# Edge scatter by sorting on one Trainium2 core: a new list of sort passes without a rotation of single columns, and smaller last pieces

## The chip, the cores and the metric

The kernel runs on one core of one Trainium2 chip. The metric is the device time of one execution in microseconds (us), taken as the median of the runs. Lower is better.

## What is computed

The reference is a message-passing step on a graph of 4096 nodes with 256 features and 262144 edges:

```python
self_out = nodes @ w_self
src_feat = nodes[edges_src]
msg = src_feat @ w_msg
agg = np.zeros((N, D), dtype=np.float32)
np.add.at(agg, edges_dst, msg)
return (self_out + agg).astype(np.float32)
```

The inputs are drawn with one fixed seed, so that the list of edges is always the same.

## The kernel before

The kernel never gathers rows. It counts, for each pair of source and destination, how many edges there are, and multiplies the counts with `Y = nodes @ w_msg`. For that the edges must be ordered, so that 128 consecutive ones fall into a narrow range of (block of 128 sources, destination). It has three stages.

**Keys and sort.** VectorE (DVE) packs each edge into one fp32 key. The 262144 keys lie as 128 partitions by 2048 columns. The table `SORT_A` is a list of compare-exchange passes `('b', m, parity)`, done by DVE (`mm`, L974: one minimum and one maximum per pass) between two buffers `XA`. In a pass of distance `m` a block of `b` columns is compared with the block `m` columns on, where `b` is the largest power of two that divides `m`. Distances over 96 go through `far_gap`, seven instructions for both parities; the rest through `near`. Between them stand the entries `('q', bb, amounts)`: TensorE (PE) rotates groups of `bb` columns over the partitions, each group by its own amount (`rotate`, L1091 to L1107). A rotation has two halves of 1024 columns. A half is two PSUM tiles of 4 groups, each filled by 4 matmuls of 128 columns in fp32 (the trace shows each as two; L1100) and copied back by ScalarE (ACT, L1104). There are eight rotations; this text calls them turns 0 to 7. The ninth `q` is done by `relayout`.

The order around a turn is written out by hand in `near`. The last two passes before a turn are done first for the first half of the columns, so that PE can turn it while DVE finishes the second half. After the turn the first two passes are done first for the first half, while PE turns the second. `warm` (L994) puts matmuls on zeros in front of a turn, each burst of three tied to a DVE instruction a given number of us ahead (`WARM`, one entry per turn). Between turns PE also does independent work (`early`: transposes, the projection `Y`, and the rows `nodes @ w_self`).

**Tail and values.** `relayout` spreads the keys anew, `tail` runs the passes of `SORT_S` on the first half of the edges (buffers `XS`); the second half (`XR`) is sorted during the main loop. PE then transposes the sorted keys and subtracts a base (L453, L462), and ACT turns the result into the int16 `vals` (L467, two instructions of 512 columns). DVE's first use of them is `pair` (L536).

**Main loop.** 2048 columns of 128 edges each, in 37 groups. `GROUPS` gives for each group the number of columns, the width `wid` of its one-hot of destinations, and the largest step to the next column. DVE (and ACT for a part, L592) builds one-hots `e_oh` (sources) and `d_oh` (destinations, `wid` wide, L601). PE multiplies them into `ring` (L628: 128 by `wid` counts a column; also 352 clearing matmuls with `zer`), ACT copies finished runs to `atr` (L655), DVE adds the spill between runs (L688), and PE multiplies the counts with `Y` (L718, L725). The wider a group, the more columns each of its matmuls and one-hots has. If one column of edges spans more than its `wid`, a flag sends the program to a slow loop over all edges at the end (`_any_edges`).

Of the kernel before, what the change touches and what calls it, by code (L numbers as in the profile page):

```python
# [9 lines left out]
P = 128  # L10
FP32 = mybir.dt.float32
# [8 lines left out]
ACTF = mybir.ActivationFunctionType  # L20
# [1 line left out]
BW = 512  # L22
SEG = 384
SHORT = 256
W = 92
NC = 64
GROUPS = [
# [7 lines left out]
]  # L35
PARTS = 2
LATE = (7, 17)
# [7 lines left out]
BEFORE, AFTER = 1, 3  # L45
FP = 96
BP = 128
WARM = [((2.7, 1.4), 3)] * 4 + [((1.6,), 3), ((2.7, 1.4), 3), ((1.6,), 3), ((1.6,), 3), ((2.7, 1.4), 3)]
FILLS = (24, 10, 10, 10, 0, 5, 0, 0, 5)
LAG = (16, 56)  # L50
RAMP = (64, 384)
# [15 lines left out]
PIECES = (512, 512, 480, 320, 224)  # L67
TOP = 32767
SORT_A = [
    ('b', 419, 0),  # L70
    ('b', 419, 1),
    ('b', 287, 0),
    ('b', 287, 1),
    ('b', 343, 0),
    ('b', 343, 1),
    ('b', 175, 0),
    ('b', 175, 1),
    ('b', 141, 0),
    ('b', 141, 1),
    ('b', 97, 0),  # L80
    ('b', 97, 1),
    ('b', 49, 0),
    ('b', 49, 1),
    ('q', 32, [108, 126, 61, 93, 118, 18, 115, 104, 48, 77, 58, 46, 7, 70, 116, 61]),
    ('b', 49, 0),
    ('b', 49, 1),
    ('b', 25, 0),
    ('b', 25, 1),
    ('q', 16, [91, 19, 26, 97, 35, 114, 42, 89, 83, 23, 118, 3, 50, 4, 17, 64]),
    ('b', 35, 0),  # L90
    ('b', 35, 1),
    ('b', 19, 0),
    ('b', 19, 1),
    ('q', 8, [116, 58, 105, 69, 107, 57, 36, 32, 125, 115, 105, 36, 76, 85, 65, 104]),
    ('b', 11, 0),
    ('b', 11, 1),
    ('b', 10, 0),
    ('b', 10, 1),
    ('q', 2, [2, 29, 75, 18, 94, 19, 8, 3, 68, 97, 94, 43, 15, 42, 52, 96]),
    ('b', 6, 0),  # L100
    ('b', 6, 1),
    ('q', 2, [110, 57, 19, 3, 2, 47, 70, 27, 104, 50, 9, 91, 21, 61, 124, 94]),
    ('b', 5, 0),
    ('b', 5, 1),
    ('b', 3, 0),
    ('b', 3, 1),
    ('q', 2, [65, 105, 76, 15, 103, 58, 124, 82, 97, 61, 78, 40, 33, 44, 18, 114]),
    ('b', 2, 0),
    ('b', 2, 1),
    ('q', 1, [49, 55, 109, 124, 1, 37, 105, 21, 18, 46, 96, 19, 46, 41, 31, 24]),  # L110
    ('b', 2, 0),
    ('b', 2, 1),
    ('q', 2, [19, 54, 43, 88, 45, 89, 44, 103, 107, 0, 94, 90, 82, 64, 24, 26]),
    ('b', 2, 0),
    ('b', 2, 1),
    ('b', 1, 0),
    ('b', 1, 1),
    ('q', 1, [48, 125, 14, 17, 54, 81, 102, 117]),
]
SORT_S = [  # L120
    (54, 0), (54, 1), (62, 0), (62, 1), (38, 0), (38, 1), (26, 0), (26, 1), (18, 0), (18, 1), (14, 0), (14, 1), (8, 0), (8, 1),
]


# [5 lines left out]
def kernel(  # L130
# [9 lines left out]
    nc = tc.nc  # L140
# [24 lines left out]
    GP = G16 // PARTS  # L165
# [52 lines left out]
    for h, m in enumerate(PIECES):  # L218
# [4 lines left out]
        q = nc.scalar if h < 4 else nc.sync  # L223
# [15 lines left out]
    for d64, s64, c in ld:  # L239
# [5 lines left out]
            out=seg[:, c], in_=dlo, func=ACTF.Copy, scale=1.0 / SEG, bias=0.5 / SEG - 6.5  # L245
        )
        nc.scalar.activation(
            out=blk[:, c], in_=slo, func=ACTF.Copy, scale=1.0 / P, bias=0.5 / P - 0.5
        )
        loaded = nc.scalar.activation(  # L250
            out=dst_p[:, c], in_=dlo, func=ACTF.Copy, scale=1.0 / (SEG - SHORT), bias=0.0
# [196 lines left out]
    tps = []  # L448
# [11 lines left out]
    for t, tp in enumerate(tps):  # L460
        for k in range(4):
            nc.tensor.matmul(  # L462
                out=tp[:, k * P:(k + 1) * P],
                lhsT=g7f[:, 4 * t + k:4 * t + k + 1].to_broadcast([P, P]), rhs=ident[:],
                start=False, stop=True, skip_group_check=True,
            )
        nc.scalar.activation(  # L467
            out=vals[:].rearrange("p (q k) -> p q k", k=GP)[:, :, 4 * t:4 * t + 4],
            in_=tp[:].rearrange("p (k q) -> p q k", k=4),
            func=ACTF.Relu, scale=-1.0, bias=top[:],  # L470
        )

    def load(c):
        regs = [nc.tensor.alloc_register(f"po{c}_{i}") for i in range(NREG)]
# [488 lines left out]
class _Sort:  # L963
# [127 lines left out]
    def rotate(self, x, y, bb, rots):  # L1091

        for h in range(2):
            sel = lambda v: v[:, FP + 1024 * h:FP + 1024 * (h + 1)].rearrange(
                "p (i g b) -> p g i b", g=8, b=bb
            )
            for t in range(2):
                tp = self.psum.tile([P, 512], FP32, name="tp_sw", tag="tp", bufs=4)
                for g in range(4):
                    self.nc.tensor.matmul(  # L1100
                        out=tp[:, g * P:(g + 1) * P], lhsT=self.turned(rots[8 * h + 4 * t + g]),
                        rhs=sel(x)[:, 4 * t + g], start=True, stop=True,
                    )
                self.nc.scalar.copy(  # L1104
                    out=sel(y)[:, 4 * t:4 * t + 4],
                    in_=tp[:].rearrange("p (g i b) -> p g i b", g=4, b=bb),
                )  # L1107

    def run(self, fill, more):
# [109 lines left out]
```

## Time and profile before

| | us |
|---|---|
| median of 3 runs | 419.08 (418.66 to 419.38) |
| profiled execution | 418.17 |
| its span, first to last instruction | 416.4 |
| around the span | 1.8 |
| busy DVE, PE, ACT, POOL in the span | 374.9, 335.5, 270.0, 43.0 |
| mean granted clock of TensorE | 0.978 |

The profiled execution is 0.91 us under the median. An engine's busy time says little by itself here, since DVE is busy for 90% of the span and PE for 81%, each the bound in another stage. What counts is which of them the others wait for, stretch by stage.

### The profile page before, as it was taken

The page shows a single profiled execution, that of the slowest core. Times are in us where ns is not written, and L with a number is a line of the kernel's source. Part 1 is how long each engine was busy: PE and PEld are TensorE (multiplying, and loading weights), DVE is VectorE, ACT ScalarE, POOL GpSimd, SP SyncE. Part 2 cuts the span into 40 slices and gives each one's busy share as a digit, 9 for nine tenths or more (in the row PEclk, how much of TensorE's full clock was granted, in tenths as well). Part 3 has the DMA queues.
Part 4 walks back from the last instruction along what each step waited for, and adds up shares of the span by engine and source line. Part 5 has one row for each costly group of instructions (what it writes and reads, how often), then busy time and mean ns, then how long its engine had stood idle before and what let it go on. Part 6 is the DMA issues. An engine that isn't in the chain of part 4 may idle for free.

```text
span 416.4 us, 10756 instructions
## 1 busy us (share of the span) xinstructions
PE 335.5 (81%) x4128; PEld 287.9 (69%) x4137; DVE 374.9 (90%) x916; ACT 270.0 (65%) x559; POOL 43.0 (10%) x172
## 2 busy tenths in 40 slices
PE   0038477876967198999999998898988999999995
PEld 0025255564845056999999998797878988898895
DVE  6999999999799989999999999989997999998851
ACT  4328154553538015889888888996876877777782
POOL 8400000000000000002011020100102030202010
PEclk9999699999999689999999999999999999999999
DMA  8690000101023200003012020230203020211212
GB/s 305 138 185 4 2 1 2 50 0 52 1 101 116 87 0 2 2 2 39 2 16 28 2 32 10 53 41 8 33 3 39 2 32 12 28 14 15 29 16 53
DMA packets 18074, 16.20 MB, mean 39 GB/s; under 512 B 3684, under 2 KB 16997, under 8 KB 18022
## 3 DMA queue, kind: packets, MB, share of 16 engines
q0 software_dynamic: 8992, 6.29, 12.7%
q1 hardware_dynamic: 8310, 7.20, 5.3%
q10 hardware_dynamic: 720, 2.00, 1.2%
q8 instruction: 34, 0.56, 0.6%
q14 instruction: 18, 0.15, 0.1%
HBM read 8.93 MB, written 8.66 MB: 42 GB/s over the span
## 4 chain that ended last, share of the span: by engine, by line
DVE 47%; PE 45%; issue 3%; ACT 3%; DMA 1%; DVEq 0%; ACTq 0%
DVE XA L974 18%; PE out_ps L718 18%; PE ring L628 17%; DVE e_oh L601 7%; PE tp_sw L1100 5%; DVE d_oh L601 5%; DVE XS L974 4%; DVE XR L974 3%; DVE off L564 3%; PE warm L994 2%; PE out_ps L725 1%; DMA d<-in_edges_dst_dram 1%; ACT XA L1104 1%; DVE atr L688 1%; ACT atr L655 1%
## 5 line engine op out<-in xcount | busy, mean ns | idle before, releaser
L655 ACT CAST atr<-ring 128x472 bf16<-128x472 f32 (+11 forms) x352 | 177.2, 553 | 45.7 <-PE ring L628 40.7
L718 PE MATMUL out_ps<-Y,atr 128*128 128x256 bf16 x1024 | 162.2, 272 | 2.9 <-DVE atr L688 2.0
L628 PE MATMUL ring<-d_oh,e_oh 128*128 128x88 bf16 (+9 forms) x2048 | 149.7, 203 | 9.9 <-issue 4.5
L628 PEld LDWEIGHTS <-e_oh 128*128 128x128 bf16 x2048 | 129.2, 97 | 16.4 <-issue 9.7
L718 PEld LDWEIGHTS <-atr 128*128 128x128 bf16 x1024 | 90.7, 97 | 10.8 <-DVE atr L688 2.3
L974 DVE TENSOR_TENSOR XA<-XA 128x510 f32<-128x510 f32 (+30 forms) x154 | 89.3, 630 | 6.9 <-ACT XA L1104 5.3
L601 DVE TENSOR_SCALAR e_oh<-off 128x1024 bf16<-128x1024 int16 (+5 forms) x254 | 87.0, 402 | 7.9 <-PE ring L628 5.2
L628 PE MATMUL ring<-zer 128*128 128x158 bf16 (+12 forms) x352 | 81.4, 231 | 0.1
L866 POOL DMA_DIRECT2D out_dram<-o_sb x30 | 28.9, 963 | 357.8 <-ACT atr L655 357.8
L601 DVE TENSOR_SCALAR d_oh<-off 128x1024 bf16<-128x1024 int16 (+5 forms) x204 | 63.9, 373 | 0.0
L1104 ACT COPY XA<-tp_sw 128x512 f32<-128x512 f32 x32 | 20.9, 654 | 41.5 <-PE tp_sw L1100 41.2
L1100 PE MATMUL tp_sw<-XA,id 128*128 128x128 f32 x256 | 36.7, 298 | 7.9 <-DVE XA L974 7.8
L1100 PEld LDWEIGHTS tp_sw<-XA,id 128*128 128x128 f32 x256 | 33.1, 194 | 13.7 <-DVE XA L974 8.7
L564 DVE TENSOR_TENSOR off<-pair,rows 128x2048 int16<-128x2048 int16 (+5 forms) x34 | 38.6, 1134 | 0.3
L628 PEld LDWEIGHTS <-zer 128*128 128x128 bf16 x352 | 34.1, 97 | 5.0 <-ACT atr L655 1.9
L994 PE MATMUL warm<-zw 128*128 128x512 bf16 x61 | 20.8, 440 | 17.5 <-DVE XS L974 9.3
L349 PE MATMUL x_ps<-id_bf,nodes_bf 128*128 128x128 bf16 x64 | 8.5, 304 | 29.3 <-DMA nodes_bf<-in_nodes_dram 28.0
L725 PE MATMUL out_ps<-Y,atr 128*88 128x256 bf16 (+7 forms) x115 | 31.2, 272 | 0.0
L688 DVE TENSOR_TENSOR atr<-atr 128x178 bf16<-128x178 bf16 (+24 forms) x100 | 23.7, 260 | 6.4 <-ACT atr L655 6.0
L349 PEld LDWEIGHTS <-nodes_bf 128*128 128x128 bf16 x64 | 6.6, 139 | 30.9 <-DMA nodes_bf<-in_nodes_dram 28.3
L321 PE MATMUL y_ps<-wcat,XT 128*128 128x256 bf16 x128 | 21.7, 278 | 6.9 <-ACT Y L325 2.8
L592 ACT ACTIVATE e_oh<-off,onesc 128x512 bf16<-128x512 uint16 (+5 forms) x36 | 24.6, 686 | 2.7 <-DVE off L564 2.7
(114 smaller groups left out, 223.3 us busy)
## 6 DMA issues: line engine op xcount, KB each, us to landing
out_dram<-o_sb POOLq DMA_DIRECT2D x30, 128.0 KB, 3.2
nodes_bf<-in_nodes_dram POOLq DMA_DIRECT2D x2, 1024.0 KB, 12.6
out_dram<-nodes_bf SPq DMA_DIRECT2D x4, 512.0 KB, 2.9
out_dram<-XA SPq DMA_DIRECT2D x4, 512.0 KB, 3.0
d<-in_edges_dst_dram SPq DMA_DIRECT2D x2, 512.0 KB, 5.5
s<-in_edges_src_dram ACTq DMA_DIRECT2D x2, 512.0 KB, 5.7
d<-in_edges_dst_dram SPq DMA_DIRECT2D x1, 480.0 KB, 9.6
s<-in_edges_src_dram ACTq DMA_DIRECT2D x1, 480.0 KB
```

The lines of the kernel that those rows point to most:

```text
L564: tt(out=v[:, 0:n // 2].rearrange("p g w (k i) -> p (g w) k i", i=2), in0=pair[:, g].rearrange("p g w i -> p (g w) i").unsqueeze(2).to_bro ...
L601: ins = tss(out=o[:, 0:n // 2, j:j + m].rearrange("p g k i -> p g (k i)"), in_=v[:, 0:n // 2, w, 0:2 * m], scalar=float((-j0 if w else ON_ ...
L628: mm = nc.tensor.matmul(out=ap, lhsT=lhsT, rhs=rhs, start=start, stop=True, skip_group_check=True,).ins
L655: ins = nc.scalar.copy(out=at[:, 0:n], in_=ring[:, b:b + n]).ins
L688: tt(out=atr[:, j:j + n, 0:m], in0=atr[:, j:j + n, 0:m], in1=atr[:, i:i + n, at:at + m], op=ALU.add,)
L718: nc.tensor.matmul(out=out_ps[:, i, :], lhsT=at[:, t * P:(t + 1) * P], rhs=Y[:, b, :], start=(b == 0 and not last and t % 2 == 0), stop=(b ...
L725: nc.tensor.matmul(out=out_ps[0:m, 0, :], lhsT=spill[:, c0:c0 + m], rhs=Y[:, b, :], start=False, stop=False, skip_group_check=True,)
L866: nc.gpsimd.dma_start(out=dst, in_=src, accum_op=ALU.add).ins,
L974: self.nc.vector.tensor_tensor(out=out, in0=in0, in1=in1, op=op),
L994: self.nc.tensor.matmul(out=w[:], lhsT=self.zw[:, 0:P], rhs=self.zw[:], start=True, stop=True).ins
L1100: self.nc.tensor.matmul(out=tp[:, g * P:(g + 1) * P], lhsT=self.turned(rots[8 * h + 4 * t + g]), rhs=sel(x)[:, 4 * t + g], start=True, sto ...
L1104: self.nc.scalar.copy(out=sel(y)[:, 4 * t:4 * t + 4], in_=tp[:].rearrange("p (g i b) -> p g i b", g=4, b=bb),)
```

## The change

There are five edits. The list `SORT_A` has other distances and amounts (same number of passes and turns), and its turn 6 rotates groups of two columns in place of single ones. `SORT_S` has other distances. `GROUPS` has other widths (from a mean of 86.4 columns to 87.7, and `W`, the widest, from 92 to 94), which follow from the new order of the edges. Each half of a rotation has three PSUM tiles, of 4, 2 and 2 groups, in place of two of 4. The bursts before the turns change: five in front of turn 0 from 6.0 us ahead, and two in front of every other turn, where turns 4, 6 and 7 had one. The activation of `vals` is done in four pieces, the first 32 columns of edges first.

```diff
-W = 92
+W = 94
...
-WARM = [((2.7, 1.4), 3)] * 4 + [((1.6,), 3), ((2.7, 1.4), 3), ((1.6,), 3), ((1.6,), 3), ((2.7, 1.4), 3)]
+WARM = [((6.0, 4.8, 3.6, 2.4, 1.2), 3)] + [((2.7, 1.4), 3)] * 8
+TURNED = ((0, 4), (4, 2), (6, 2))
...
-    ('b', 419, 0),
-    ('b', 419, 1),
...
+    ('b', 812, 0),
+    ('b', 812, 1),
...
-    ('q', 1, [49, 55, 109, 124, 1, 37, 105, 21, 18, 46, 96, 19, 46, 41, 31, 24]),
+    ('q', 2, [64, 80, 21, 16, 104, 59, 44, 35, 47, 1, 40, 49, 125, 101, 28, 24]),
...
-        nc.scalar.activation(
-            out=vals[:].rearrange("p (q k) -> p q k", k=GP)[:, :, 4 * t:4 * t + 4],
-            in_=tp[:].rearrange("p (k q) -> p q k", k=4),
-            func=ACTF.Relu, scale=-1.0, bias=top[:],
-        )
+    for q in (slice(0, 32 // GP), slice(32 // GP, P)):
+        for t, tp in enumerate(tps):
+            nc.scalar.activation(
+                out=vals[:].rearrange("p (q k) -> p q k", k=GP)[:, q, 4 * t:4 * t + 4],
+                in_=tp[:].rearrange("p (k q) -> p q k", k=4)[:, q],
+                func=ACTF.Relu, scale=-1.0, bias=top[:],
+            )
...
-            for t in range(2):
-                tp = self.psum.tile([P, 512], FP32, name="tp_sw", tag="tp", bufs=4)
-                for g in range(4):
+            for g0, n in TURNED:
+                tp = self.psum.tile([P, 512], FP32, name="tp_sw", tag="tp", bufs=4)[:, 0:n * P]
+                for g in range(n):
                     self.nc.tensor.matmul(
-                        out=tp[:, g * P:(g + 1) * P], lhsT=self.turned(rots[8 * h + 4 * t + g]),
-                        rhs=sel(x)[:, 4 * t + g], start=True, stop=True,
+                        out=tp[:, g * P:(g + 1) * P], lhsT=self.turned(rots[8 * h + g0 + g]),
+                        rhs=sel(x)[:, g0 + g], start=True, stop=True,
                     )
                 self.nc.scalar.copy(
-                    out=sel(y)[:, 4 * t:4 * t + 4],
-                    in_=tp[:].rearrange("p (g i b) -> p g i b", g=4, b=bb),
+                    out=sel(y)[:, g0:g0 + n],
+                    in_=tp.rearrange("p (g i b) -> p g i b", g=n, b=bb),
                 )
```

The distances over 96, which set the length of the far passes, were 419, 287, 343, 175, 141, 97 and are 812, 323, 279, 269, 163, 97. The first far passes on DVE, before (the last number is columns, or blocks by columns of a block; `x2` is two equal rows):

```order
L974 TENSOR_TENSOR XA_93<-XA_92 128x815
L974 TENSOR_TENSOR XA_92<-XA_92 128x605
L974 TENSOR_TENSOR XA_93<-XA_92 128x210
L974 TENSOR_TENSOR XA_93<-XA_92,XA_93 128x605 x2
L974 TENSOR_TENSOR XA_93<-XA_92 128x209 x2
L974 TENSOR_TENSOR XA_92<-XA_93 128x881
```

and with the change:

```order
L977 TENSOR_TENSOR XA_93<-XA_92 128x155x4
L977 TENSOR_TENSOR XA_92<-XA_92 128x53x4
L977 TENSOR_TENSOR XA_93<-XA_92 128x102x4
L977 TENSOR_TENSOR XA_93<-XA_92,XA_93 128x53x4 x2
L977 TENSOR_TENSOR XA_93<-XA_92 128x101x4 x2
L977 TENSOR_TENSOR XA_92<-XA_93 128x863
```

The number of instructions is the same; those of the first pair are shorter.

The copies of turns 5 and 6 on ACT, before (`tp_sw` with its number is the PSUM tile; the size is groups by rows of blocks by columns of a block):

```order
L1104 COPY XA0_92<-tp_sw_890 128x4x64x2
L1104 COPY XA0_92<-tp_sw_896 128x4x64x2
L1104 COPY XA0_92<-tp_sw_902 128x4x64x2
L1104 COPY XA0_92<-tp_sw_908 128x4x64x2
L1104 COPY XA1_93<-tp_sw_930 128x4x128
L1104 COPY XA1_93<-tp_sw_936 128x4x128
L1104 COPY XA1_93<-tp_sw_942 128x4x128
L1104 COPY XA1_93<-tp_sw_948 128x4x128
```

and with the change:

```order
L1107 COPY XA0_92<-tp_sw_926 128x4x64x2
L1107 COPY XA0_92<-tp_sw_932 128x2x64x2
L1107 COPY XA0_92<-tp_sw_936 128x2x64x2
L1107 COPY XA0_92<-tp_sw_940 128x4x64x2
L1107 COPY XA0_92<-tp_sw_946 128x2x64x2
L1107 COPY XA0_92<-tp_sw_950 128x2x64x2
L1107 COPY XA1_93<-tp_sw_974 128x4x64x2
L1107 COPY XA1_93<-tp_sw_980 128x2x64x2
L1107 COPY XA1_93<-tp_sw_984 128x2x64x2
L1107 COPY XA1_93<-tp_sw_988 128x4x64x2
L1107 COPY XA1_93<-tp_sw_994 128x2x64x2
L1107 COPY XA1_93<-tp_sw_998 128x2x64x2
```

Turn 6 has the form of turn 5, and the last copy of each half is half as long. PE's own order is unchanged but for the bursts.

## Rows read from the trace of the kernel before

**Rows 1.** Windows by stage: length, then busy PE, PEld, DVE, ACT, POOL, clock, DMA

```profile
19.18:46.65 27.47, 12.09 (x80) 8.42 (x80) 26.92 (x42) 11.53 (x24) 1.15 (x2) 0.94 0.59 77
46.65:126.08 79.43, 62.32 (x391) 46.31 (x397) 72.89 (x125) 35.14 (x76) 0.00 (x0) 0.98 0.08 27
...
202.00:262.00 60.00, 57.58 (x840) 53.43 (x838) 58.43 (x147) 51.09 (x104) 5.46 (x6) 1.00 0.13 17
262.00:411.00 149.00, 139.91 (x2085) 127.69 (x2086) 129.07 (x392) 117.19 (x243) 20.62 (x21) 1.00 0.19 24
```

**Rows 2.** The page's chain that ended last, shares of the span by line

```profile
DVE XA L974 18%; PE out_ps L718 18%; PE ring L628 17%; DVE e_oh L601 7%; PE tp_sw L1100 5%; DVE d_oh L601 5%; DVE XS L974 4%; DVE XR L974 3%; DVE off L564 3%; PE warm L994 2%; PE out_ps L725 1%; DMA d<-in_edges_dst_dram 1%; ACT XA L1104 1%; DVE atr L688 1%; ACT atr L655 1%
```

**Rows 3.** Timeline of DVE between the turns: start, length, work, [idle before it]

```profile
52.57 10.52 DVE L974 TENSOR_TENSOR XA<-XA 128x511 f32<-128x511 f32 x16 [0.66 <-ACT XA L1104]
63.34 10.49 DVE L974 TENSOR_TENSOR XA<-XA 128x511 f32<-128x511 f32 x16 [0.25 <-ACT XA L1104]
...
93.12 7.84 DVE L974 TENSOR_TENSOR XA<-XA 128x515 f32<-128x515 f32 x12 [0.26 <-ACT XA L1104]
101.25 5.56 DVE L974 TENSOR_TENSOR XA<-XA 128x510 f32<-128x510 f32 x12 [0.29 <-ACT XA L1104]
109.09 3.03 DVE L974 TENSOR_TENSOR XA<-XA 128x510 f32<-128x510 f32 x8 [2.28 <-ACT XA L1104]
112.82 5.14 DVE L974 TENSOR_TENSOR XA<-XA 128x510 f32<-128x510 f32 x8 [0.70 <-ACT XA L1104]
118.33 7.84 DVE L974 TENSOR_TENSOR XA<-XA 128x514 f32<-128x514 f32 x12 [0.36 <-ACT XA L1104]
```

**Rows 4.** DVE instructions by form: busy, mean ns of one

```profile
L974 DVE TENSOR_TENSOR XA<-XA 128x976 f32<-128x976 f32 x1 | 1.2, 1177 | 0.0
L974 DVE TENSOR_TENSOR XA<-XA,XA 128x605 f32<-128x605 f32 x2 | 1.6, 788 | 0.0
L974 DVE TENSOR_TENSOR XS<-XS 128x256 f32<-128x256 f32 x4 | 1.5, 420 | 0.0
L601 DVE TENSOR_SCALAR d_oh<-off 128x1024 bf16<-128x1024 int16 x135 | 49.1, 418 | 0.0
```

**Rows 5.** Timeline of PE around turns 1, 4 and 6

```profile
57.97 1.67 PE L994 MATMUL warm<-zw 128*128 128x512 bf16 x5
...
86.42 0.81 PE L994 MATMUL warm<-zw 128*128 128x512 bf16 x3
87.47 2.10 PE L1100 MATMUL tp_sw<-XA,id 128*128 128x128 f32 x16 [0.24 <-DVE XA L974]
...
102.91 0.81 PE L994 MATMUL warm<-zw 128*128 128x512 bf16 x3
104.01 7.65 PE L1100 MATMUL tp_sw<-XA,id 128*128 128x128 f32 x32 [0.30 <-DVE XA L974]
```

**Rows 6.** Timeline of ACT after turn 4: a copy of 512 columns, one of 256

```profile
92.50 0.59 ACT L1104 COPY XA<-tp_sw 128x512 f32<-128x512 f32 x1 [0.25 <-PE tp_sw L1100]
92.98 0.38 ACT L325 COPY nodes_bf<-y_ps 128x256 f32<-128x256 f32 x1
```

**Rows 7.** Windows ahead of turn 0 and turn 5, columns as in rows 1

```profile
41.80:46.60 4.80, 0.00 (x0) 0.00 (x0) 4.70 (x8) 0.37 (x1) 0.00 (x0) 0.67 0.00 0
...
92.30:98.40 6.10, 3.22 (x17) 1.29 (x15) 5.73 (x10) 2.16 (x6) 0.00 (x0) 1.00 0.26 89
```

**Rows 8.** The values: timelines of ACT and DVE, and a short activation by form

```profile
153.12 1.52 ACT L467 ACTIVATE vals<-tp_sw,top 128x512 int16<-128x512 f32 x2 [17.45 <-PE tp_sw L462]
...
154.67 0.18 DVE L536 TENSOR_SCALAR pair<-vals 128x32 int16<-128x32 int16 x1 [1.09 <-ACT vals L467]
...
L498 ACT ACTIVATE rel_q<-XR,g7f 128x128 int16<-128x128 f32 x8 | 2.9, 404 | 0.0
```

**Rows 9.** PE's matmuls into the ring by form: busy, mean ns of one

```profile
L628 PE MATMUL ring<-d_oh,e_oh 128*128 128x83 bf16 x288 | 20.2, 201 | 0.6 <-issue 0.2
...
L628 PE MATMUL ring<-d_oh,e_oh 128*128 128x90 bf16 x192 | 14.5, 205 | 0.3 <-issue 0.2
```

More of the change, by code (lines that the diff above doesn't have):

```diff
@@ L69 @@
 SORT_A = [
-    ('b', 419, 0),
-    ('b', 419, 1),
[L72 to L79, printed above, removed]
+    ('b', 812, 0),
+    ('b', 812, 1),
+    ('b', 323, 0),
+    ('b', 323, 1),
+    ('b', 279, 0),
+    ('b', 279, 1),
+    ('b', 269, 0),
+    ('b', 269, 1),
+    ('b', 163, 0),
+    ('b', 163, 1),
     ('b', 97, 0),
     ('b', 97, 1),
[L82 to L102, printed above, removed]
+    ('b', 54, 0),
+    ('b', 54, 1),
+    ('q', 32, [102, 55, 115, 44, 27, 73, 103, 20, 45, 68, 53, 40, 23, 87, 82, 41]),
+    ('b', 82, 0),
+    ('b', 82, 1),
+    ('b', 51, 0),
+    ('b', 51, 1),
+    ('q', 16, [3, 61, 58, 1, 27, 117, 122, 84, 122, 53, 62, 24, 36, 4, 35, 72]),
+    ('b', 29, 0),
+    ('b', 29, 1),
+    ('b', 21, 0),
+    ('b', 21, 1),
+    ('q', 8, [67, 92, 79, 68, 20, 82, 28, 50, 104, 1, 86, 8, 103, 12, 43, 58]),
+    ('b', 13, 0),
+    ('b', 13, 1),
+    ('b', 9, 0),
+    ('b', 9, 1),
+    ('q', 2, [43, 88, 94, 55, 63, 89, 96, 71, 82, 54, 7, 112, 117, 88, 14, 22]),
+    ('b', 7, 0),
+    ('b', 7, 1),
+    ('q', 2, [118, 5, 84, 86, 8, 61, 102, 88, 87, 50, 27, 114, 111, 40, 66, 10]),
     ('b', 5, 0),
@@ L106 @@
     ('b', 3, 1),
-    ('q', 2, [65, 105, 76, 15, 103, 58, 124, 82, 97, 61, 78, 40, 33, 44, 18, 114]),
+    ('q', 2, [50, 26, 89, 49, 88, 116, 9, 77, 55, 8, 84, 40, 38, 89, 14, 108]),
     ('b', 2, 0),
     ('b', 2, 1),
-    ('q', 1, [49, 55, 109, 124, 1, 37, 105, 21, 18, 46, 96, 19, 46, 41, 31, 24]),
+    ('q', 2, [64, 80, 21, 16, 104, 59, 44, 35, 47, 1, 40, 49, 125, 101, 28, 24]),
     ('b', 2, 0),
     ('b', 2, 1),
-    ('q', 2, [19, 54, 43, 88, 45, 89, 44, 103, 107, 0, 94, 90, 82, 64, 24, 26]),
+    ('q', 2, [52, 47, 92, 72, 102, 25, 97, 88, 110, 3, 59, 101, 35, 54, 99, 120]),
     ('b', 2, 0),
@@ L117 @@
     ('b', 1, 1),
-    ('q', 1, [48, 125, 14, 17, 54, 81, 102, 117]),
+    ('q', 1, [35, 94, 7, 63, 40, 91, 54, 72]),
 ]
 SORT_S = [
-    (54, 0), (54, 1), (62, 0), (62, 1), (38, 0), (38, 1), (26, 0), (26, 1), (18, 0), (18, 1), (14, 0), (14, 1), (8, 0), (8, 1),
+    (42, 0), (42, 1), (70, 0), (70, 1), (34, 0), (34, 1), (30, 0), (30, 1), (18, 0), (18, 1), (14, 0), (14, 1), (8, 0), (8, 1),
 ]
```

14 rows, old and new, of the table GROUPS are left out of this document.

## The prediction

> **What bounds the kernel now.** I read the windows by stage first. Through the sort DVE is busy for 26.92 of 27.47 us while it does the far passes and for 72.89 of 79.43 in the stage of the turns, while PE is busy for less than half of the first and has long gaps in the second; in the main loop DVE leads between 202 and 262 us (58.43 of 60) and PE after that (139.91 of 149, DVE 129.07) [rows 1]. The chain that ended last says the same: the passes on XA and XS and the one-hots are DVE's, `ring` and `out_ps` are PE's, 17% and 18% of the span [rows 2]. So a column less in a DVE pass before 150 us counts in full, and a column more in the ring counts wherever PE leads. Next I read DVE's timeline for the places where the sort does not compute. It idles once per turn, for about 0.25 us (turns 2 and 3 have 0.24 each, as turn 1 has 0.25), for 0.66 at turn 0, and for 2.28, 0.70 and 0.36 around turns 6 and 7, each time until a copy by ACT [rows 3]. PE's timeline gives the cause of the large ones: turn 6, of single columns, takes 32 matmuls in 7.65 us, where a half of another turn takes 16 in 2.10 [rows 5].
>
> **The passes.** The far list loses 962 columns of instructions (21652 before, 20690 now, in 42 instructions both times); the near passes gain 129, the tail 96. A column costs (1177 - 788) / 371 = 1.05 ns [rows 4]. Nothing else runs on that path, so this is 737 x 1.05 = **0.77 us less**. Blocks of four and of two columns replace single ones in some passes. The tail's blocks of eight fall on the same line (420 ns for 256 columns, and 788 - 349 x 1.05 = 422), so for those I take the same price.
>
> **Turn 6.** Between 101.25 and 118.33 us, 17.08 us, DVE waits 2.28 + 0.70 + 0.36 = 3.34 us for copies [rows 3]. Where DVE does not wait, an instruction starts some 0.08 us before the end of the last, which the three waits also cost: 3.6 us in all. With groups of two columns turn 6 is like turn 4, where the first half (from 87.47, 2.10 long) is turned while DVE does the second and DVE does not wait for it. So 3.6 us go, but not all: the bursts. A burst of three issues in 0.64 (five take 1.67 and three 0.81, so 0.215 a matmul). PE does its work in order, and there is little room: at turn 6 the single burst starts at 102.91, so PE is free at 103.55, and the turn is ready at 104.01. Two bursts hold PE until 104.19, 0.18 late [rows 5]. At turn 4 they start at 86.42 and hold PE until 87.70, 0.23 behind the 87.47 at which it could start. At turn 7 the half before the burst starts later by what turn 6 was late, and I get about 0.4. Shorter last copies (next part) take 0.2 back each time; DVE, which comes 0.2 earlier itself, then waits about 0.23 at each of the three. For turns 6 and 7 that leaves 3.6 - 0.45 = **3.15 us less**. The ends: 3.6 if the bursts delay nothing, and 2.6 if each costs a whole burst more.
>
> **Smaller last tiles.** A half's last copy now has 256 columns. A copy of 512 takes 0.59, one of 256 0.38 [rows 6], and the last matmuls of the half end when they did, so DVE goes on 0.2 us earlier, wherever it waits for that copy: turns 0, 1, 2, 3 and 5, 1.0 us. The two more copies per half lie on ACT, which is idle between the copies. At turn 4 the 0.26 of the second half [rows 3] goes with its 0.08, and a wait of 0.23 behind the bursts comes: 0.1. Turn 0 waits 0.4 longer than turn 1, and TensorE ran at the lower of its two levels in part of the stretch before it (mean granted clock 0.67 while PE was idle) [rows 7]. Five bursts from 6 us ahead follow the projection within half a us, so that the long idle stretch is gone; I take the whole 0.4. Together **1.5 us less**; ends 0.6 and 2.0.
>
> **The values.** DVE waits 1.09 us until the second of two activations, 153.12 to 154.64, ends [rows 8]. Now it waits for two pieces of 16 columns. The first is hidden in the time in which ACT waits for the second tile's matmuls. The second takes at most the 0.40 us of the form with 128 columns, in place of 0.69 [rows 8]; the slope between the two gives some 0.3. So **0.4 us less**; ends 0.29 and 0.6. The long pieces end later than before, by about 0.8 us, and DVE needs them only for the second split of `vals`, over 4 us later. [...]
>
> **The wider groups.** The mean width goes from 86.4 to 87.7: 2512 more columns in 2048 matmuls, and 510 more in the clearing ones. By the forms of 83 and 90 columns a column costs (205 - 201) / 7 = 0.57 ns; the two means are rounded, so I take 0.5: 1.5 us on PE [rows 9]. PE leads in about three quarters of the main loop, which makes 1.15. In the rest DVE leads, and of its 2480 more elements of `d_oh` at no more than 418 / 1024 = 0.41 ns [rows 4], 1.0 us, a quarter counts, 0.2. Together **1.3 us more**; ends 0, if all of it falls into the idle 9 us that PE has after 262 [rows 1], and 2.5, if both count everywhere.
>
> **The sum.** -0.77 - 3.15 - 1.5 - 0.4 + 1.3 = -4.5 us. Against the profiled execution's own 418.17 this is 413.7; it stands 0.9 below the median of 419.08, against which it would be 414.6. Part of that 0.9 may be turn 0, whose clock came back just in time in this execution; the change would end that difference. I take 414.1.
>
> **The rivals.** *A low clock at turn 0.* The new bursts come in groups of three with pauses. If the clock falls in spite of them, and is low when turn 0 starts, its matmuls take twice 2.1 us, 2.1 longer than forecast for the first half: 416.2. Against it: between 92.30 and 98.40 PE was busy for 3.22 of 6.10 us with such pauses, and the granted clock stayed at 1.00 [rows 7]; the new bursts make about as much. For it: the clock did fall before turn 0 when PE stood idle. [...] Chance 0.14.
>
> *More is hidden.* The bursts delay nothing (0.7 us) and the wider groups fall into idle time (1.3): 414.1 - 2.0 = 412.1. For it speaks that PE idles 9 us of its own last stage, against it that the chain runs through the ring there [rows 1, 2]. Chance 0.15.
>
> *The table does not fit.* This one ends on the other side. The widths and steps in `GROUPS` are right only for the order that the new list makes of this draw. One column of 128 edges that spans a destination more than its `wid` sets the flag, and the slow loop runs: 2048 rounds. Of each only its DVE instructions, at 0.4 us for a small one [rows 4], would make over 2000 us. It decides at a single column. The list has passes over all distances, the draw is fixed, and the widths that I get by carrying the passes out on that draw are those of the table; so 0.01. That the change does not do what it says otherwise is not possible for the passes, whose lengths are in the program.
>
> **How the numbers follow.** The forecast has 0.68, with 412.9 to 415.6 as its own range from the ends above, of which not all fall on one side. The other case below (0.15) and the low clock (0.14) lie at 412.1 and 416.2; the range of 412.0 to 416.4 takes in both centres and half of what lies beyond. A measurement of this kernel can tell about 0.2%, 0.8 us, from no change. Every case but the last lies more than that below 419.08, so faster has 0.96; 0.02 each are left for no change and for slower, where several small delays and the last rival are.
>
> **What would show it.** Right: far passes that end about 1.0 us earlier; no copy over 0.6 us and 16 matmuls a half at turn 6; DVE waits of about 0.05 us at turns 0, 1, 2, 3, 5 and of about 0.2 at turns 4, 6 and 7, each behind six `warm` matmuls; `pair` 0.4 us nearer to the last subtraction on PE; a main loop about 1.3 us longer from `pair` to the end. Wrong: a granted clock under 1.00 at turn 0, a main loop as long as before or longer by over 2.5 us, or DVE waits at turns 4, 6 and 7 that are gone or over half a us.

## The result and the profile after

The changed kernel takes **408.44 us** (median of four executions, 407.44 to 409.74), the kernel before, run beside it, 418.87 (418.18 to 419.38): a ratio of 0.9754, 95% interval 0.9715 to 0.9792. The forecast was 414.1 with a range of 412.0 to 416.4, so the gain is more than twice the one forecast. The profiled execution took 409.74 us, its span 408.0. It is 1.3 above its median, the one of before (418.17) 0.7 below the 418.87; of the 10.4 us between the medians the two profiles show 8.4. Ratios in this text leave out executions that took over 1.5% longer than the fastest of their kernel, which are two of `e5_before_pad18` and one of `c4_old_lists`.

The windows of the kernel after come first: the far passes and the turns as in [rows 1], then a stretch ahead of turn 0, which answers to [rows 7], and one near the end of the tail. Columns as in [rows 1].

```profile
18.71:45.30 26.59, 15.79 (x88) 9.58 (x89) 26.00 (x43) 11.58 (x24) 0.94 (x2) 1.00 0.60 79
45.30:120.37 75.07, 59.33 (x402) 43.74 (x406) 72.91 (x125) 33.96 (x92) 0.00 (x0) 1.00 0.09 29
38.00:45.40 7.40, 5.94 (x19) 2.09 (x18) 7.26 (x13) 2.27 (x7) 0.00 (x0) 1.00 0.00 0
142.00:144.00 2.00, 1.94 (x7) 0.79 (x6) 1.93 (x7) 0.00 (x0) 0.00 (x0) 0.61 0.00 0
```

The far passes are 0.9 us shorter. Their clock of 1.00 can't be taken at its word: in this trace the clock is on record only from 44.6 us on, and windows show 1.00 for what is not on record. The 512-column matmuls of the bursts start 0.38 to 0.43 us apart up to 44.04 and 0.21 apart from 44.73 on. The trace of before has two levels of the granted clock, 0.50 and 1.00; there such matmuls start 0.38 to 0.43 us apart at 0.50 (43.5 to 50.3 us) and 0.21 apart at 1.00 (from 86.42, ahead of turn 4), so TensorE was at the lower level until about 44.6 and at the higher when turn 0 began, at 48.13. DVE in the stage of the turns is as busy as before (72.91 and 72.89 us) in 4.4 us less. The chain of the kernel after, shares of the span by line, against [rows 2]:

```profile
PE out_ps L721 24%; PE ring L631 23%; DVE XA L977 19%; DVE XS L977 4%; DVE e_oh L604 3%; PE out_ps L728 3%; PE tp_sw L1103 3%; DVE d_oh L604 2%; PE warm L997 2%; ACT XA L1107 2%; DVE off L567 1%; DMA d<-in_edges_dst_dram 1%; DVE XR L977 1%;
```

PE's two lines of the main loop have grown from 35% to 47%. DVE's timeline (start, length, work, idle before it) now has only two waits that the view sets apart, where before it had nine (seven of them in [rows 3]):

```profile
45.06 42.82 DVE L977 TENSOR_TENSOR XA<-XA 128x48 f32<-128x48 f32 x70
88.11 16.01 DVE L977 TENSOR_TENSOR XA<-XA 128x511 f32<-128x511 f32 x28 [0.24 <-ACT XA L1107]
104.39 16.06 DVE L977 TENSOR_TENSOR XA<-XA 128x510 f32<-128x510 f32 x28 [0.27 <-ACT XA L1107]
```

PE's timeline around turns 4 and 6 tells why these two stay. Each follows a turn of 16 matmuls that comes right behind six of `warm`, so PE was late; at turn 6 the 32 matmuls in 7.65 us of [rows 5] have become twice 16 in about 2 us.

```profile
84.22 1.67 PE L997 MATMUL warm<-zw 128*128 128x512 bf16 x6
85.72 1.95 PE L1103 MATMUL tp_sw<-XA,id 128*128 128x128 f32 x16
...
100.44 1.67 PE L997 MATMUL warm<-zw 128*128 128x512 bf16 x6
101.94 1.95 PE L1103 MATMUL tp_sw<-XA,id 128*128 128x128 f32 x16
104.27 2.02 PE L1103 MATMUL tp_sw<-XA,id 128*128 128x128 f32 x16 [0.38 <-DVE XA L977]
```

The values, ACT's timeline, against [rows 8]:

```profile
147.50 0.27 ACT L470 ACTIVATE vals<-tp_sw,top 128x16 int16<-128x16 f32 x1 [17.56 <-PE tp_sw L463]
148.34 0.84 ACT L470 ACTIVATE vals<-tp_sw,top 128x16 int16<-128x16 f32 x2 [0.56 <-PE tp_sw L463]
```

`pair` starts at 148.64 (154.67 before). Counted from the first far pass (18.71; 19.18 before), the sort and the values take 129.93 us in place of 135.49, **5.56 less**. The prediction's first four terms make 5.82. The main loop, from `pair` to the end of the span, takes 259.3 us in place of 261.7: **2.4 less, where 1.3 more was forecast**. So the question is the main loop, in which the change only widened groups.

### The profile page after: what moved, and what is told of

Read it like the earlier page. It is cut to its first block, busy times and chain, and to the rows that moved or that the text cites. A ratio compares the mean times of both kernels' runs of the same rounds, so it can differ in the third digit from the quotient of the medians.

```text
span 408.0 us, 10819 instructions
## 1 busy us (share of the span) xinstructions
PE 336.9 (83%) x4145; PEld 288.6 (71%) x4155; DVE 374.9 (92%) x916; ACT 269.1 (66%) x577; POOL 43.1 (11%) x172
## 4 chain that ended last, share of the span: by engine, by line
PE 55%; DVE 37%; ACT 3%; issue 3%; DMA 1%; DVEq 0%; ACTq 0%
PE out_ps L721 24%; PE ring L631 23%; DVE XA L977 19%; DVE XS L977 4%; DVE e_oh L604 3%; PE out_ps L728 3%; PE tp_sw L1103 3%; DVE d_oh L604 2%; PE warm L997 2%; ACT XA L1107 2%; DVE off L567 1%; DMA d<-in_edges_dst_dram 1%; DVE XR L977 1%; DVE XA L260 1%; DVE XA L255 1%
## 5 line engine op out<-in xcount | busy, mean ns | idle before, releaser
L658 ACT CAST atr<-ring 128x471 bf16<-128x471 f32 (+11 forms) x352 | 177.2, 555 | 43.5 <-PE ring L631 38.3
L631 PE MATMUL ring<-d_oh,e_oh 128*128 128x87 bf16 (+10 forms) x2048 | 150.3, 204 | 5.1 <-DVE d_oh L604 2.0
L977 DVE TENSOR_TENSOR XA<-XA 128x510 f32<-128x510 f32 (+33 forms) x154 | 89.4, 630 | 2.6 <-ACT XA L1107 0.5
L1107 ACT COPY XA<-tp_sw 128x256 f32<-128x256 f32 (+1 forms) x48 | 19.7, 448 | 38.0 <-PE tp_sw L1103 37.7
L1103 PE MATMUL tp_sw<-XA,id 128*128 128x128 f32 x256 | 32.4, 278 | 7.0 <-DVE XA L977 6.5
L1103 PEld LDWEIGHTS tp_sw<-XA,id 128*128 128x128 f32 x256 | 30.0, 190 | 11.3 <-DVE XA L977 9.2
L997 PE MATMUL warm<-zw 128*128 128x512 bf16 x78 | 24.6, 425 | 14.8 <-DVE XS L977 9.4
L728 PE MATMUL out_ps<-Y,atr 128*89 128x256 bf16 (+6 forms) x115 | 31.3, 272 | 0.0
L691 DVE TENSOR_TENSOR atr<-atr 128x174 bf16<-128x174 bf16 (+24 forms) x100 | 23.6, 262 | 5.8 <-ACT atr L658 5.3
L997 PEld LDWEIGHTS <-zw 128*128 128x128 bf16 x87 | 8.4, 104 | 27.7 <-DVE XS L977 9.7
```

Of the source, the lines that this page charges most:

```text
L631: mm = nc.tensor.matmul(out=ap, lhsT=lhsT, rhs=rhs, start=start, stop=True, skip_group_check=True,).ins
L658: ins = nc.scalar.copy(out=at[:, 0:n], in_=ring[:, b:b + n]).ins
L691: tt(out=atr[:, j:j + n, 0:m], in0=atr[:, j:j + n, 0:m], in1=atr[:, i:i + n, at:at + m], op=ALU.add,)
L728: nc.tensor.matmul(out=out_ps[0:m, 0, :], lhsT=spill[:, c0:c0 + m], rhs=Y[:, b, :], start=False, stop=False, skip_group_check=True,)
L977: self.nc.vector.tensor_tensor(out=out, in0=in0, in1=in1, op=op),
L997: self.nc.tensor.matmul(out=w[:], lhsT=self.zw[:, 0:P], rhs=self.zw[:], start=True, stop=True).ins
```

## What the trace of before showed in the main loop

PE's waits of the kernel before from 155 to 412 us (line, what it waited for, total, times, longest), those without a releaser:

```profile
PE ring L628 <- issue: 4.5, 9, 1.2
...
PE out_ps L718 <- issue: 0.4, 1, 0.4
```

And of the kernel after:

```profile
PE out_ps L721 <- issue: 2.3, 4, 1.2
...
PE ring L631 <- issue: 1.6, 4, 0.5
```

"issue" is time in which nothing that the profile knows held PE. One such place of before, in PE's timeline:

```profile
318.34 0.20 PE L628 MATMUL ring<-d_oh,e_oh 128*128 128x89 bf16 x1
319.76 0.38 PE L628 MATMUL ring<-d_oh,e_oh 128*128 128x89 bf16 x5 [1.23 <-issue]
```

It falls inside a row of equal matmuls, and in the trace neither the matmul at 319.76 nor its weight load waits for a semaphore. The queues of the page of before have one that no line of the kernel feeds (packets, MB, share):

```profile
q8 instruction: 34, 0.56, 0.6%
```

These are 34 loads of 16 KB, and PE's program, as compiled, has 8251 instructions, about 243 for each load. In the trace one load lasts from 317.06 to 318.49, and PE goes on at 319.76. I numbered the ring's and `out_ps`'s matmuls by their place in PE's program (weight loads and waits counted too) and took, for each, the time since the start of the one before, less its columns at the rate of the `warm` matmuls at a granted clock of 1.00 (0.21 us for 512) and 5 ns, which are an estimate (ring matmuls of 88 columns start 40 ns apart in the median, 3 more than this rate gives). Places where the profile shows PE waiting for another engine are left out. In the kernel before seven pauses of 0.5 to 1.4 us stand at instructions 4338, 4850, 5363, 5875, 6130, 7154 and 7411: all within 1 of the same remainder, 243, modulo 256. In each of the seven PE goes on 1.17 to 1.49 us after the end of the load that ran just before. I call the places with that remainder borders. Over the 28 borders of the main loop the pauses sum to **7.5 us before and 5.1 after**, which is the 2.4 us by which the loop is shorter. What the change did to them: the ring began at PE's instruction 712 and begins at 749, mostly through the 18 added `warm` matmuls with a weight load each, so every border falls on other work. The traces show this without the numbering: counted from the ring's first matmul, pauses stand before numbers 1747, 2241 and 2488 in the kernel before and before 1730, 2223 and 2470 in the kernel after, 17 or 18 matmuls earlier.

## The experiments

Theory A: the new widths and steps shorten the loop themselves. Theory B: the borders of PE's program moved. Theory C: chance from execution to execution. Later F: the bursts act on the main loop in another way. The pauses, the loop and the clock are read from the one execution of each kernel that was traced; the medians are of all. All ratios are to the kernel before, run beside each. The expectations have 8.8 us of pauses for before, since they count 1.29 at a border (instruction 5108) where PE also waits for DVE; the tables below leave such places out everywhere.

### One part of the change at a time

`e1_lists_only`: the kernel before with `SORT_A`, `SORT_S`, `GROUPS` and `W` of the change.

> The kernel before with the new sort lists, widths and steps, and nothing else of the change. The sort should give 0.8 us for the columns and 3.6 for turn 6, as its bursts stay single: 4.4 less until `pair`. Theory A (the widths and steps of the new table make the main loop shorter): the main loop from `pair` to the end is about 2.4 us shorter, as in the changed kernel, so 6.8 less in all, about 412. Theory B (PE's 36 added instructions ahead of the main loop move its instruction loads, and so its stalls): without them the main loop is longer by up to 1.3, so 3.1 to 4.4 less, 414.5 to 415.8. Theory C (the main loop varies by this much from execution to execution): between the two, with main loops that overlap those of the kernel before.

416.36 us, ratio 0.9944 (0.9926 to 0.9962). The sort and values are 3.6 shorter, the main loop 265.0, 3.3 *longer* than before. Theory A falls.

`e2_old_bursts`: the changed kernel with `WARM` of before.

```
-WARM = [((6.0, 4.8, 3.6, 2.4, 1.2), 3)] + [((2.7, 1.4), 3)] * 8
+WARM = [((2.7, 1.4), 3)] * 4 + [((1.6,), 3), ((2.7, 1.4), 3), ((1.6,), 3), ((1.6,), 3), ((2.7, 1.4), 3)]
```

> The changed kernel with the warming bursts of the kernel before: 18 matmuls fewer, in other places. In the sort turn 0 loses its long burst (0.4 to 0.6 us more, clock low before it), and turns 4, 6 and 7 lose the 0.2 that PE held them up (0.6 to 0.7 less): about even. Theory A: the main loop stays as in the changed kernel, time 408.0 to 409.0. Theory B: the main loop loses its gain of 2.4 us, time 410.5 to 411.5. Theory C: anywhere between.

415.47 us, 0.9913 (0.9889 to 0.9937). Until `pair` it is 0.3 behind the changed kernel, in the main loop (263.9) 4.5. PE's waits in the loop (155 to 412 us):

```profile
PE ring L631 <- issue: 6.8, 11, 1.4
```

`e4_bursts_only`: the kernel before with the new `WARM`.

> The kernel before with the new bursts alone: 36 more PE instructions ahead of the main loop, and the same lists. In the sort turn 0 gains 0.4 to 0.6 (no low clock ahead of it), turns 4, 6 and 7 lose 0.2 each: 0 to 0.2 longer until `pair`. Theory A: main loop as before, 418.9 to 419.2 in all. Theory B: main loop 2.4 shorter or more (the lists cost it 1.3), 415.5 to 417. Theory C: in between.

413.88 us, 0.9872 (0.9846 to 0.9897): half of the whole gain, from bursts that do no work. The sort takes what it took (135.49 us from the first far pass to `pair`, as before), the main loop 257.3, 4.4 less. So the same 18 matmuls are worth 4.4 us in the main loop with the old lists and 4.5 with the new. Theory C falls too: the changed kernel took 407.4 to 409.7 us, with the old bursts 414.6 to 417.0.

B's forecasts for these three had the sign right, but not the size: 414.5 to 415.8 for `e1_lists_only`, 410.5 to 411.5 for `e2_old_bursts`, 415.5 to 417 for `e4_bursts_only`. They took the 2.4 us between the two loops for the worth of the bursts. At nearly the same borders the new lists and widths make the loop longer, by 2.1 us (`e2_old_bursts` against before) and by 2.0 (the changed kernel against `e4_bursts_only`), so the bursts gave more than 2.4.

`e3_wider`: the kernel before with 4 added to the width of every group, and `W = 96`.

> The kernel before with every width 4 columns larger, sort and order untouched: prices a column alone. 2400 matmuls of the ring x 4 columns x 0.5 ns are 4.8 us on PE, and the elements of d_oh some 3.3 us on DVE. The recorded price (PE counts in three quarters of the loop, DVE in the rest): 4.4 us longer, about 423.5. Theory D (width falls mostly into idle time of the main loop): 0 to 1.5 us longer. Theory A says nothing of it unless 4 columns change the grouping of the merges, which they do not, since neighbours stay equal or unequal.

420.55 us, 1.0027 (1.0009 to 1.0045); the profiled loop is 2.0 longer, at about the same pauses (7.8 and 7.5). A column more costs under half of what I priced.

### Nothing but the place of the borders

Matmuls that do nothing are put ahead of the sort, where PE stands idle:

```
     sort = _Sort(nc, tc, psum_sort, XA, XS, id2, zw)
+    sort.pad(18)
...
+    def pad(self, n):
+        w = self.psum.tile([P, 512], FP32, name="warm", tag="warm", bufs=1)
+        for _ in range(n):
+            self.nc.tensor.matmul(
+                out=w[:, 0:64], lhsT=self.zw[:, 0:P], rhs=self.zw[:, 0:64], start=True, stop=True
+            )
```

`e5_before_pad18`: that, on the kernel before.

> The kernel before with 18 idle matmuls of 64 columns ahead of the first transposes, while PE has nothing to do: 36 more PE instructions, so that the ring begins at instruction 748 of PE's program (712 before, 749 in the changed kernel). Theory B (blocks of 256 instructions are loaded into PE's program one after the other; 36 more move every border between blocks to other work): sort as before, borders stall 3 to 5 us in all instead of 8.8, main loop 257 to 258, 414.0 to 415.5 in all. Theory F (the bursts do something else in the sort that the main loop feels: its clock, its buffers): main loop as before, 419.2.

416.53 us, 0.9942 (0.9917 to 0.9968): 0.6% less than the kernel before, clear of no change as B says, but about half of what the bursts gain at the same place of the borders. The execution that was traced took 424.54 us, the longest of 13. Its loop takes 268.0 us and ran at the lower clock from 255.3 to 258.8 and from 320.2 to 323.6 (mean granted clock 0.97 from 200 to 260 us, 0.98 from 320 to 420), so it is not in the table below. At the same borders as in `e4_bursts_only` its pauses are longer: the longest is 2.04 us, and the load before it started 0.21 us ahead of the border, where in `e4_bursts_only` the load started 2.00 ahead and the pause is 0.83. PE's timeline at this border, here and in `e4_bursts_only`:

```profile
318.72 0.39 PE L719 MATMUL out_ps<-Y,atr 128*128 128x256 bf16 x2 [1.87 <-issue]
...
316.06 0.38 PE L718 MATMUL out_ps<-Y,atr 128*128 128x256 bf16 x2 [0.67 <-issue]
```

So the place of the borders alone does not fix the pauses; what else does is open.

`e6_after_pad110`: the changed kernel with `sort.pad(110)`.

> The changed kernel with 110 such matmuls: 220 instructions more, which together with the 36 of the change make a whole block, so that the ring begins where it began before (instruction 969, which is 713 and one block of 256; 713 in the changed kernel with the old bursts). All bursts and all of the sort are the changed kernel's. Theory B: borders stall 10 us as with the old bursts, main loop about 263.9, 412.5 to 413.5 in all. Theory F: no difference to the changed kernel, 408.4.

416.62 us, 0.9931 (0.9905 to 0.9957): 220 idle instructions ahead of all work cost the changed kernel over 7 us, with the sort unchanged (130.1 us from the first far pass to `pair`). F alone can't explain that, since all bursts are there. The loss is larger than the 4.5 expected, and the loop of 266.6 is 2.8 us longer than that of `e2_old_bursts`, which has the same lists and its ring at the same place modulo 256; so F, or another cause beside the place, may hold for a part.

`e9_after_pad256`: `sort.pad(256)`, 512 instructions, twice the distance of the borders.

> The changed kernel with 256 matmuls of 64 columns ahead of the sort, 512 PE instructions: two whole blocks, so every border falls on the same work as in the changed kernel. If the place of the border alone decides: main loop 259 to 260, 408.4 to 409.5 in all. If the length of the program or what went before decides: any other value, as with 110 matmuls, where the loop was 2.8 us longer than with the old bursts at the same borders. In the row of small matmuls itself, where nothing else runs, a border should show as a pause of 1 us or more, 256 instructions apart.

410.76 us, 0.9784 (0.9752 to 0.9816), an interval that overlaps that of the changed kernel. The loop takes 259.4, the pauses 5.2 us: what the changed kernel has. More than twice as many idle instructions as in `e6_after_pad110`, and the loss is gone, so here it is the place and not the number. In PE's timeline the row of idle matmuls shows a border by itself, where no other work is near:

```profile
3.11 8.55 PE L998 MATMUL warm<-zw 128*128 128x64 bf16 x223 [3.11 <-POOL ones_sent L281]
13.40 1.12 PE L998 MATMUL warm<-zw 128*128 128x64 bf16 x33 [1.74 <-issue]
```

A load runs from 10.88 to 11.98, and PE goes on 1.42 us after its end. Only one of the two borders that I expected shows; 256 instructions ahead of this one PE does not pause.

`e8_after_pad64`, `e10_after_pad16`, `e11_after_pad96`, `e12_after_pad40`, and later `c2_after_pad6` and `c3_after_pad120`: the same with other numbers.

> The changed kernel with 64 matmuls of 64 columns ahead of the sort: borders half a block away from where they were. Theory B: the sum of the stalls at borders is some other value between 3 and 11 us, and the main loop differs from the changed kernel's by about the same amount (254.5 to 263), with all borders of the trace again at one place modulo 256 instructions. Theory F: 408.4.

> The changed kernel with 16 such matmuls: borders 32 instructions earlier in the work. Main loop = about 253.5 us and the stalls at borders (so it came out in the runs so far: 252 to 255 and 3.5 to 14.5): 256 to 264 us, so 405 to 413 in all, with stalls summed from its own trace that agree with its loop within 1.5 us. A theory in which the lists make the difference: 408.4.

> The changed kernel with 96 such matmuls, 192 instructions. As for 16: main loop = 253.5 and the stalls at its borders within 1.5 us, 405 to 415 in all.

> The changed kernel with 40 such matmuls, 80 instructions. As for 16: main loop = 253.5 and the stalls at its borders within 1.5 us, 405 to 415 in all. One of the three may come out below the changed kernel.

> The changed kernel with 6 small matmuls ahead of the sort: borders 12 instructions earlier in the work. If the good place is wide: main loop within 1.5 us of 259.3. If what stands just ahead of a border decides: 261 to 266, as at the other places. Either way loop = 254 and the stalls at the borders within 1.5 us.

> The changed kernel with 120 small matmuls, 240 instructions: borders 16 instructions later in the work. As with 6: a main loop within 1.5 us of 259.3 if the good place is wide, 261 to 266 if not, and loop = 254 and the stalls within 1.5 us.

With the others, ordered by the remainder of the instruction at which the ring begins (pauses at borders, main loop and their difference from the profiled execution, us):

```
kernel               ring at  mod 256  pauses   loop  loop-pauses  median of all
e10_after_pad16          781       13     9.1  263.9        254.8         412.97
e12_after_pad40          829       61    11.9  266.5        254.6         414.13
e8_after_pad64           877      109     9.8  262.4        252.6         413.10
e11_after_pad96          941      173    11.4  265.9        254.5         417.75
e1_lists_only            711      199     9.1  265.0        256.0         416.36
before                   712      200     7.5  261.7        254.2         418.87
e3_wider                 712      200     7.8  263.8        256.0         420.55
e2_old_bursts            713      201     9.9  263.9        253.9         415.47
e6_after_pad110          969      201    11.8  266.6        254.8         416.62
c3_after_pad120          989      221     8.6  263.1        254.5         413.89
e4_bursts_only           747      235     3.5  257.3        253.9         413.88
after                    749      237     5.1  259.3        254.2         408.44
e7_single_pad9           749      237     6.0  259.9        253.9         410.17
c1_single_longtail       749      237     5.5  259.4        253.9         409.49
c4_old_lists             749      237     4.7  259.4        254.6         413.47
e9_after_pad256         1261      237     5.2  259.4        254.2         410.76
c2_after_pad6            761      249     5.6  259.4        253.8         414.35
```

The pauses go from 3.5 to 11.9 us, the loop from 257.3 to 266.6, and the difference stays between 252.6 and 256.0, whatever the lists, widths and bursts; in 14 of the 17 it is 253.8 to 254.8. The totals of `e6_after_pad110` and `e11_after_pad96` came out above what was expected (412.5 to 413.5 and 405 to 415). The change put the borders at the best place that was tried, and none of the other numbers of idle matmuls beats it: the good place reaches from 235 to 249, and 221 is outside. Even there it isn't sure: `e5_before_pad18`, at 236, took 414.8 to 424.5 us, and `c2_after_pad6` took 410.0 and 410.4 us in two executions and 414.1 to 415.2 in four. The profile is of one of the short ones; what the long ones did isn't seen.

### The lists and the bursts with the borders held

`c4_old_lists`: the changed kernel with the four tables of before; its ring begins at 749 too.

> The changed kernel with the sort lists, widths and steps of before, its ring at the same instruction 749. Sort: smaller last tiles and values give 1.5 to 1.9 us against before, turn 6 stays: `pair` at about 153. Main loop: if the width costs what 4 columns more cost on the kernel before (2.0 us for 4, so 0.6), 0.6 shorter than the changed kernel's apart from its stalls, 253.5 and stalls of 3.5 to 5: 257 to 258.7, 411.5 to 413 in all. If the recorded price holds (1.3): 0.7 less. If the lists make the main loop shorter by themselves: 261 or more, 415.

413.47 us, 0.9837 (0.9805 to 0.9869). The loop takes 259.36 us, the changed kernel's 259.31. The equal times don't show that lists and widths cost nothing, since TensorE ran at the lower level, a granted clock of 0.50, in a part of this loop:

```profile
316.70:320.10 3.40, 3.40 (x30) 2.88 (x28) 2.18 (x7) 1.65 (x4) 0.84 (x1) 0.50 0.38 43
```

From the 2240th matmul of the loop to the 2266th it took 3.22 us, where `e4_bursts_only`, with the same lists, took 1.75 at the higher level. Without this 1.5 us the loop would be 257.9, 1.4 shorter than the changed kernel's, and its difference to the pauses 253.1. (`e12_after_pad40` has such a stretch too, from 384.0 to 387.4. In all four of them, with the two of `e5_before_pad18`, PE had stood still for 1.7 to 2.0 us shortly before; after a pause of 2.37 us in `e11_after_pad96` the clock did not fall.) So new lists and widths together cost the loop 1.4 to 2.0 us at the good place, part of it as pauses, and what the lists gain is all in the sort: 133.79 us from the first far pass to `pair`, 3.9 more than in the changed kernel.

`e7_single_pad9`: the changed kernel with single bursts at turns 4, 6 and 7, and 9 idle matmuls ahead of the sort for those taken away.

> The changed kernel with single bursts at turns 4, 6 and 7 as before, and 9 matmuls of 64 columns ahead of the sort in place of the 9 that this takes away: PE's program is as long as in the changed kernel (749). Theory B: main loop as in the changed kernel; the sort loses the 0.2 us or so by which the bursts held up each of the three turns: 407.7 to 407.9. If the long burst at turn 0 were not all that the clock needs, a stretch at a lower clock shows at turns 5 to 8 and the time is 409 or more.

410.17 us, 0.9768 (0.9742 to 0.9794), as the changed kernel. The minimum of the last values starts 0.47 us earlier, counted from the first far pass, but `pair` only 0.04. TensorE's clock was low in the tail and came back later here, at 144.3 us (143.6 in the changed kernel); a window, columns as in [rows 1]:

```profile
142.00:144.00 2.00, 2.00 (x6) 1.07 (x6) 1.93 (x7) 0.00 (x0) 0.00 (x0) 0.50 0.00 0
```

The transposes of the values started at the lower level, a granted clock of 0.50, and took 2.28 us in place of 1.95, and DVE waited for what comes behind them.

`c1_single_longtail`: the same, with one burst more ahead of them.

```
-        self.warm(marks[-2], (4.0, 2.7, 1.4), 4)
+        self.warm(marks[-2], (5.2, 4.0, 2.7, 1.4), 4)
```

> The changed kernel with single bursts at turns 4, 6 and 7 and, at the end of the tail, one burst more, 1.2 us earlier than the first of before, so that TensorE is at the higher level again when the transposes of the first values start; 5 small matmuls ahead of the sort keep the ring at instruction 749. If the late clock took the 0.4 us that the single bursts gave: `pair` 0.4 earlier than in the changed kernel, main loop 259 to 260, 408.0. If not: as with the single bursts alone, 408.4 to 409.

409.49 us, 0.9736 (0.9705 to 0.9767). The clock is back in time:

```profile
142.00:144.00 2.00, 1.86 (x12) 1.15 (x10) 1.97 (x6) 0.00 (x0) 0.00 (x0) 1.00 0.00 0
```

and `pair` starts 0.50 us earlier than in the changed kernel, from the first far pass. In the whole time that can't be told apart from the changed kernel, whose interval overlaps: executions of one program differ by 2 us and more. That the main loop's pauses make this difference is not shown, as one execution of each was traced.

## Why the prediction was wrong, point by point

The sum for the sort came out nearly right; what failed is the price of the bursts, which the sum took from the sort alone (last item).

- **The passes**: 0.77 less forecast, of it 1.0 in the far passes. These take 0.88 us less (26.59 and 27.47 in the windows), the tail 0.09 more. Right.
- **Turn 6**: 3.15 less forecast. The stretch from turn 5 to the resume after turn 7's first wait went from 17.08 to 14.07 us (98.56 to 112.63), 3.0 less. The delay behind the bursts is there, 0.24 at turn 4, 0.27 at turn 6, 0.14 at turn 7, of the size forecast. The 0.215 us of a `warm` matmul does not follow from the two rows that the prediction names for it (0.86 us for two more would be 0.43 each), but at the higher clock they do start 0.21 to 0.23 us apart, so the term stands.
- **Smaller last tiles**: 1.5 less forecast. Turn 0 gave 0.59, turns 1, 2, 3 and 5 together 0.70, turn 4 0.05: 1.3. Of these, DVE waits for more than 0.08 us only at turn 4. The low clock at turn 0, a rival, did not come: its first 16 matmuls take 2.05 us, from 48.13, at a granted clock of 1.00. Before, the clock came back at 50.3, not "just in time" but 0.8 us into the turn.
- **The values**: 0.4 less forecast, 0.41 measured (`pair` 6.03 earlier, the minimum 5.62). The short activation takes 0.27 us, where the slope between the two longer forms gave some 0.3.
- **The wider groups**: 1.3 more forecast. `e3_wider` has 2.0 for 4 columns, so an estimate of 0.6 for the 1.3 columns that the mean grew. New lists and widths together make the loop 1.4 to 2.1 us longer at like borders, but much of it is in the pauses. So the term was of the right sign and perhaps twice too large; it is not what made the forecast wrong.
- **The bursts in the main loop**: this step failed. The sum priced the added bursts only by what they delay in the sort and put their effect behind it at nothing. But the main loop held 7.5 us of pauses of PE that no engine causes, and 18 more matmuls with their weight loads moved all borders of PE's program to other work. That is worth 4.4 us by `e4_bursts_only` against before and 4.5 by the changed kernel against `e2_old_bursts`. It turned a loop forecast 1.3 us longer into one 2.4 shorter.

"More is hidden" was the rival on the right side, but without the mechanism, and its 412.1 was still too high. That the forecast missed on the gainful side is luck of the place: nothing in the change was meant to move the borders.

The rows that would have warned stood in the profile of before: 4.9 us of "issue" idle on PE inside rows of ready matmuls, and a queue of 34 instruction loads of 16 KB. Numbered by their place in PE's program, seven pauses of the main loop lie within 1 of one remainder modulo 256, and the pauses at the borders sum to 7.5 us before and to 11.9 in `e12_after_pad40`.

What stays open: what decides how early a load starts. Of the 28 borders of the kernel before 20 pass with a pause under 0.4 us and without a wait for DVE, so I take the load to have been there in time; in the changed kernel a load that starts 6.36 us ahead of its border costs nothing and one that starts 0.83 ahead costs 1.40. At the same border of the same work the load started 2.00 us ahead in `e4_bursts_only` and 0.21 in the traced execution of `e5_before_pad18`, so the place does not settle it. Which stretch of instructions sets this was not tried, and so no run says how to choose a place other than by trying it. That the executions of one program fall into groups is not explained either.

## What to carry to other kernels

An instruction that only keeps an engine warm still takes room in that engine's program: here the 18 added `warm` matmuls with their weight loads are 36 of the 37 instructions by which the ring begins later on PE (712 to 749), and the pauses fell on other work. Where a trace shows pauses of this kind, at a fixed distance in an engine's program (256 instructions on PE here, 7.5 us in all), count them before pricing the rest, and price any edit that adds or removes instructions on that engine as moving all later ones. When two versions differ by a few us in a stage that neither edit touches, pad one of them in an idle place until both begin that stage at the same instruction modulo this distance, and compare again over several executions, since even at equal borders `e4_bursts_only` and `e5_before_pad18` differ by 0.7%. A gain that comes from this is luck of the place and may go with the next edit; here it is some 4.5 of the 8.4 us between the two profiles, of which the new lists and widths took 2.0 back.

## What was not expected of the hardware

A load of 16 KB takes 0.9 to 1.9 us in the trace of before, and in the seven pauses of before PE goes on no sooner than 1.17 us after its end. Of the two low stretches of before, the one ahead of turn 0 (granted clock 0.5 from 43.5 to 50.3 us) does not come with one long burst, with which the clock rises at 44.6 and stays up through all turns (1.00 from 44.6 to 126). But a row of `warm` matmuls can run at the lower level itself until the work it is for begins: in `e7_single_pad9` the twelve at the end of the tail began at 138.07, and the transposes behind them, at 143.59, still started at the lower level (0.50 from 142 to 144); in the changed kernel, with twelve that began some 5.3 us ahead of the transposes, TensorE was back at the higher level at 143.6, just before them at 143.80.
